# Start addresses of split weights, and a smaller table of cosines and sines, in a hybrid attention layer

## The chip, the cores and the metric

The kernel runs on one core of one Trainium2 chip. The core has TensorE (PE in the profile, with its weight loads shown as PEld), VectorE (DVE), ScalarE (ACT), GpSimd (POOL) and SyncE (SP), which here only issues transfers. The metric is the device time of one execution in microseconds (us). Durations of single instructions are given in ns.

## The reference

One encoder layer on 512 tokens of width 2048, with 16 learned tokens put ahead (528 in all), everything in float32:

```python
hn = rmsnorm(h, pre_norm_g)
proj = hn @ w_in                       # 2048 -> queries, keys, values, gates of A and B
# mixer A: 8 query heads, 2 key/value heads of 128; RMSNorm of q and k, axial rotation, softmax
ya = gqa_axial_mixer(qa, ka, va, ...) * silu(ga)
# mixer B: 8 heads of two 64-wide halves; softmax(s1) - lam * softmax(s2), distance penalty, RMSNorm
yb = diff_attn_mixer(qb, kb, vb, ...) * silu(gb)
y  = concat([ya, yb]) @ w_out
out = (h + rmsnorm(y, post_norm_g))[:, 16:, :]

def rope_half(x, ang):                 # applied to each 64-wide half of a head
    x1, x2 = split(x, 2)               # 32 and 32
    return concat([x1 * cos(ang) - x2 * sin(ang), x2 * cos(ang) + x1 * sin(ang)])
```

## The kernel before

**Products in split form.** Every float32 operand of a large product is held as two rounded parts, high and low: `wh`, `wl` for weights, `xh`, `xl` for the normalised input. A product is three matmuls, high by high, low by high and high by low (`three`). A weight block of 128 x 1024 arrives in `st` by a transfer on SP's queue (`wload`), ACT writes its high part `wh`, and DVE subtracts to get `wl` (`wsplit`). `st`, `wh` and `wl` each have three buffers in pool `wp`. `fetch` keeps two to three blocks ahead of PE, in the order of the list `todo`.

**Projections.** `dense_T` multiplies 128 output columns of the weights (the stationary operand, 128 x 128 a matmul) by all of x (the moving operand), over 16 steps k of the input width. For keys and values the moving operand has all 528 tokens, in two runs of 264 columns (`KEYS`), so one k is six matmuls of 264 columns. For queries of B and gates it has the 512 real tokens in one run (`REAL`), three matmuls of 512 columns a k. The projections of A's queries (`queries_A`) and of the output have the weights as the moving operand. `T_VB`, `T_KB`, `T_KA` and `T_VA` name the blocks of values and keys of B and A in `w_t`; `col` gives the two sources of one block of 128 columns.

**Order.** PE's order is written out by the program: a planner (`Lanes`) counts an estimated time as it emits projections, and lets generators of the attention heads run at set lags in between (scores `sc`, transposes `tr`, products with the values `pv`). The order on ACT and DVE comes from a scheduler that knows priorities: weight splits have `high_priority`. SP's loads stand in program order.

**Places in memory.** Operands lie in SBUF, each partition of which is one row of bytes. In the built program the tiles of x start 192 bytes behind a multiple of 256, so that the keys' two runs start at 192 and 224 and the run of real tokens at 0 (modulo 256); `wh` and `wl` start at 0. The keys of the B heads (`s1`, `s2`, `s` in the profile) have four buffers, at 64, 128, 192 and 0, and their queries (`q`, `l`) start at 64.

**The rotation.** For A, `head_norm` scales each head, and `rope` rotates: x times cosines, plus the exchanged halves of x times sines. The tables `cosT` and `sinT` have 128 columns per token: each value of the 32 cosines of an axis stands twice, and each sine stands once with a minus and once with a plus. `rope` runs twice for the keys of A (`kn`, at 473 and 504 us) and eight times for its queries (`qn`, from 552 to 656 us).

Of the kernel before, what the change touches and what calls it, by code (L numbers as in the profile page):

```python
# [11 lines left out]
F32R = mybir.dt.float32r  # L12
F16 = mybir.dt.float16
AF = mybir.ActivationFunctionType
ALU = mybir.AluOpType
AX = mybir.AxisListType

P = 128
# [5 lines left out]
TT = SEQ // P  # L24
# [16 lines left out]
T_KA, T_VA, T_GA, T_QB, T_KB, T_VB, T_GB = 0, 2, 4, 12, 20, 28, 36  # L41


class Lanes:
# [13 lines left out]
    def mm(self, out, lhsT, rhs, start, stop):  # L58
        n = int(np.prod(rhs.shape[1:]))
        us = max(n, 256) / 2370.0  # L60
        if rhs.dtype == F32:
            us = 4 * max(n, 128) / 2370.0
        self._add(self.nc.tensor.matmul(out, lhsT, rhs, start=start, stop=stop), us)  # L63
# [45 lines left out]
def kernel(ctx: ExitStack, tc: tile.TileContext, xT, xn, xm, w_s, w_t, w_q, w_o,  # L109
                             gpre, gq, gk, lams, gsub, gpost, ident_d, cos_d, sin_d, dist_d, out):  # L110
    nc = tc.nc
# [6 lines left out]
    wp = ctx.enter_context(tc.tile_pool(name="wp", bufs=3))  # L118
# [5 lines left out]
    ap = att.enter_context(tc.tile_pool(name="ap", bufs=2))  # L124
# [6 lines left out]
    def ctile(shape, name, dt=F32, src=None, pool=cst):  # L131
        t = pool.tile(shape, dt, name=name, tag=name, bufs=1)
        if src is not None:
            load(t, src)
        return t
# [5 lines left out]
    def load(out, in_):  # L141

        tc.keep_in_program_order(nc.sync.dma_start(out=out, in_=in_))


    def wload(src, n=1024, dma=nc.sync.dma_start, parts=1):
        st = wp.tile([P, 1024], F32, name="st", tag="st")
        ws = None
        for i in range(parts):
            c = slice(i * n // parts, (i + 1) * n // parts)  # L150
            dma(out=st[:, c], in_=src if parts == 1 else src[:, c])
            ws = wsplit(st, c, ws)
        return ws

    def wsplit(st, c=slice(0, 1024), ws=None):
        wh, wl = ws or [wp.tile([P, 1024], F32R, name=n, tag=n) for n in ("wh", "wl")]
        with tc.high_priority(rank[0]):
            nc.scalar.activation(wh[:, c], st[:, c], AF.Copy)  # L158
            nc.vector.tensor_tensor(out=wl[:, c], in0=st[:, c], in1=wh[:, c].bitcast(F32),  # L159
                                    op=ALU.subtract)  # L160
        return wh, wl
# [35 lines left out]
    todo, chunks = [], []  # L197

    def fetch(ahead=2):
        while todo and len(chunks) <= ahead:  # L200
            src = todo.pop(0)
            chunks.append(src() if callable(src) else wload(src))
        return chunks.pop(0)
# [15 lines left out]
    def col(ct):  # L219
        return [w_t[ct, :, k0:k0 + 8, :] for k0 in (0, 8)]  # L220


    start = [KEYS, REAL, REAL]
    first = [[pd.tile([P, 512], F32, name="pd", tag="pd") for _ in segs] for segs in start]
    for k0 in range(0, KT, 2):
        xload(k0)
        wh, wl = wload(w_s[k0 // 2], 768, load, 2 if k0 == 0 else 1)
        xload(k0 + 1)
        for k in (k0, k0 + 1):
            for i, (segs, pss) in enumerate(zip(start, first)):  # L230
                c = slice((i + 3 * (k - k0)) * P, (i + 3 * (k - k0) + 1) * P)
# [12 lines left out]
                                op0=ALU.mult, op1=ALU.add)  # L244
        nc.gpsimd.tensor_tensor(out=dst, in0=dst, in1=mhalf[:rows, :dst.shape[1]], op=ALU.pow)  # L245

    todo += col(T_VB)
    chunks += [wload(todo.pop(0)) for _ in range(2)]


    ssx = ctile([P, TT, 2], "ssx")
# [3 lines left out]
    for t in range(TT + 1):  # L255
        for j in range(2):
            st = ap.tile([P, 1024], F32, name="xns", tag="ph" if j else "pl")
            rows = P if t < TT else NM
            src = xn[t * P:(t + 1) * P, :] if t < TT else xm
# [12 lines left out]
                            op0=ALU.mult)  # L272
# [3 lines left out]
    def spread():  # L276
# [4 lines left out]
        mm(ps[:, :NM], ones[:NM, :], dg[:NM, :NM], start=True, stop=True)  # L281
        nc.vector.tensor_copy(out=rB[:, :NM], in_=ps[:, :NM])

    cosT = ctile([P, TT, P], "cosT", src=cos_d, pool=ap)
    sinT = ctile([P, TT, P], "sinT", src=sin_d, pool=ap)
    gqB = ctile([P, P], "gqB", src=gq, pool=ap)
    gkB = ctile([P, P], "gkB", src=gk, pool=ap)
    pad(cst, "spad", 160)
# [2 lines left out]
                            op0=ALU.mult)  # L291
# [291 lines left out]
    def head_norm(raw, n, g, rows=P):  # L583

        ss = ap.tile([P, 4], F32, name="ssh", tag="ssh", bufs=4)
        for i in range(n):
            jk = ap.tile([P, P], F32, name="jk", tag="jk", bufs=1)
            nc.scalar.activation(jk[:rows], raw[:, i, :], AF.Square, accum_out=ss[:rows, i:i + 1])  # L588
        rstd(ss[:rows, :n], ss[:rows, :n], P, rows)
        for i in range(n):  # L590
            nc.vector.scalar_tensor_tensor(out=raw[:, i, :], in0=raw[:, i, :],
                                           scalar=ss[:rows, i:i + 1], in1=g[:rows], op0=ALU.mult,
                                           op1=ALU.mult)

    def rope(x, cos, sin):

        t2f = ap.tile([P, NT], F32, name="t2", tag="tT")
        t2 = t2f[:, :4 * P].rearrange("p (n a r) -> p n a r", n=4, a=2)
        xv = x.rearrange("p n (a r) -> p n a r", a=2)
        sv = sin.rearrange("p n (a r) -> p n a r", a=2)  # L600
        nc.vector.tensor_tensor(out=t2[:, :, :, 0:32], in0=xv[:, :, :, 32:64],
                                in1=sv[:, :, :, 0:32], op=ALU.mult)
        nc.vector.tensor_tensor(out=t2[:, :, :, 32:64], in0=xv[:, :, :, 0:32],
                                in1=sv[:, :, :, 32:64], op=ALU.mult)
        nc.vector.tensor_tensor(out=x, in0=x, in1=cos, op=ALU.mult)
        nc.vector.tensor_tensor(out=x, in0=x, in1=t2f[:, :4 * P].rearrange(
            "p (n d) -> p n d", n=4), op=ALU.add)

    def keys_A(pss):
# [8 lines left out]
        def turn():  # L618
            tr = ptr.tile([P, 512], F32, name="tr", tag="tr")
            for c in range(TT):  # L620
                transpose(tr[:, c * P:(c + 1) * P], kf[:, NM + c * P:NM + (c + 1) * P], ident)
            for c in range(TT):
                nc.scalar.activation(kn[:, c, :], tr[:, c * P:(c + 1) * P], AF.Copy,
                                     scale=rt[:, c:c + 1])
            yield LAG["bank"]
            tr = ptr.tile([P, 512], F32, name="tr", tag="tr")
            transpose(tr[:NM, :P], kf[:, 0:NM], ident)
            nc.scalar.activation(km[:, 0, :], tr[:NM, :P], AF.Copy, scale=rm)
            head_norm(kn, TT, gkB)
            head_norm(km, 1, gkB, NM)  # L630
            rope(kn, cosT, sinT)
            yield LAG["rope"]
            tr = ptr.tile([P, 512], F32, name="tr", tag="tr")
            for c in range(TT):
                transpose(tr[:, c * P:(c + 1) * P], kn[:, c, :], ident)
            hi(kh[:, NM:], tr)
            lo(kl[:, NM:], tr, kh[:, NM:])
            yield LAG["bank"]
            tr = ptr.tile([P, 512], F32, name="tr", tag="tr")
            transpose(tr[:, :NM], km[:, 0, :], ident[:NM, :NM])  # L640
            hi(kh[:, :NM], tr[:, :NM])
            lo(kl[:, :NM], tr[:, :NM], kh[:, :NM])
# [3 lines left out]
    def queries_A(g):  # L646

        pss = [pd.tile([P, 512], F32, name="pd", tag="pd") for _ in range(TT)]
        for k0 in range(0, KT, 2):
            wh, wl = fetch()  # L650

            for k, ts in [(k, h) for h in ((0, 1), (2, 3)) for k in (k0, k0 + 1)]:
                c = slice((k - k0) * 512, (k - k0 + 1) * 512)
                for t in ts:
                    ts_ = slice(NM + t * P, NM + (t + 1) * P)
                    mm(pss[t], xh[k][:, ts_], wh[:, c], start=(k == 0), stop=False)
                    mm(pss[t], xl[k][:, ts_], wh[:, c], start=False, stop=False)
                    mm(pss[t], xh[k][:, ts_], wl[:, c], start=False, stop=(k == KT - 1))
                    lanes.poll()
        res = []  # L660
        for t in range(TT):
            tag = "ql" if g == 0 else "fr" if t < 2 else "f"
            qn = ap.tile([P, 4, P], F32, name="qn", tag=tag, bufs=2 if tag == "fr" else 4)
            nc.scalar.activation(qn.rearrange("p n d -> p (n d)"), pss[t], AF.Copy,
                                 scale=rt[:, t:t + 1])
            res.append(qn)

        def turn():
            for t, qn in enumerate(res):
                head_norm(qn, 4, gqB)  # L670
                rope(qn, cosT[:, t:t + 1, :].broadcast_to([P, 4, P]),
                     sinT[:, t:t + 1, :].broadcast_to([P, 4, P]))
                yield LAG["norm"]

        return res, lanes.spawn(turn(), 0.0)


    for h in range(NH):
        if h and h not in LATE:
            todo += col(T_GB + h)  # L680
        if h + 1 < NH:
            todo += col(T_VB + h + 1) + col(T_KB + h + 1) + col(T_QB + h + 1)
    for i in range(2):
        todo += col(T_KA + i) + col(T_VA + i)
    for grp in range(2):
        todo += [w_q[grp, :, k0:k0 + 2, :] for k0 in range(0, KT, 2)]
        for h in GATES[grp]:
# [95 lines left out]
    for grp in range(2):  # L783
        qn, q_task = queries_A(grp)
        for i in range(4):
            h = 4 * grp + i
# [12 lines left out]
    op = ctx.enter_context(tc.tile_pool(name="op", bufs=1, side="right", reuse_waits="tile"))  # L799
# [70 lines left out]
    t1, t2, t3, t4 = [], [], [], []  # L870
# [243 lines left out]
```

## Time and profile before

| What | before |
|---|---|
| median of 3 runs | 928.91 us (928.5 to 929.88) |
| the profiled execution | 928.50 us |
| its span, first to last instruction | 926.7 us |
| mean granted clock of TensorE | 0.998 |
| PE busy, matmuls | 912.6 us, 5498 |
| DVE / ACT / POOL busy | 571.0 / 491.8 / 116.6 us |
| bytes moved by DMA | 128.11 MB |

The profile shows one execution on the chip. The span is 1.8 us shorter than the execution's time. A row of a group gives line, engine, operation, output and inputs by the program's names, partitions x elements, count, then busy us and mean ns, then the idle time of the engine before it and what ended it. A row of the timeline gives start and duration in us; in brackets stands idle time before it. A row of the chain gives start and length of one piece of the work that ended last. `pd`, `po`, `sc`, `tr` and `pv` are sums in PSUM of a projection, of the output projection, of scores, of transposes and of products with values.

### The profile page before, as it was taken

What the parts mean: (1) busy time and instruction counts of PE and PEld (TensorE: products, weight loads), DVE (VectorE), ACT (ScalarE), POOL (GpSimd) and SP (SyncE); (2) the same over time, 40 slices, a digit from 0 to 9 for tenths busy, and PEclk for the clock granted to TensorE, in tenths of its full rate; (3) what the DMA queues carried; (4) which work ended last, traced back from release to release, by engine and by line L of the source; (5) the groups of instructions that cost most, each with busy time, mean ns of one, the idle gap of its engine ahead of it and who ended that gap; (6) DMA issues with size and microseconds to landing.
All of it is one profiled execution on the core that took longest, in us unless ns stands there. A gap on an engine that the chain in (4) does not pass through costs nothing.

```text
span 926.7 us, 14251 instructions
## 1 busy us (share of the span) xinstructions
PE 912.6 (98%) x5498; PEld 807.3 (87%) x5498; DVE 571.0 (62%) x1012; ACT 491.8 (53%) x853; POOL 116.6 (13%) x164
## 2 busy tenths in 40 slices
PE   9999999999999999999999999999999999999996
PEld 7989898998989899898999888887888888888884
DVE  6276675757557486665765236447745574654797
ACT  6765474737456374654754254337555673524661
POOL 0001110110101111010010011114111111200110
PEclk9999999999999999999999999999999999999999
DMA  9755534544636355222223323221222162865884
GB/s 333 261 158 148 137 105 125 156 119 145 160 94 189 94 151 156 69 87 86 80 69 87 106 73 111 69 80 58 76 73 80 57 216 83 274 215 167 299 304 181
DMA packets 43252, 128.11 MB, mean 138 GB/s; under 512 B 5008, under 2 KB 8976, under 8 KB 42928
## 3 DMA queue, kind: packets, MB, share of 16 engines
q1 hardware_dynamic: 39776, 115.66, 37.4%
q0 software_dynamic: 3264, 11.54, 6.7%
q8 instruction: 43, 0.70, 0.3%
q14 instruction: 25, 0.20, 0.1%
q10 hardware_dynamic: 144, 0.01, 0.0%
HBM read 118.80 MB, written 25.17 MB: 155 GB/s over the span
## 4 chain that ended last, share of the span: by engine, by line
PE 90%; DVE 4%; ACT 2%; issue 2%; DMA 1%; POOL 1%; SPq 0%; DVEq 0%; ACTq 0%; POOLq 0%
PE pd L63 58%; PE po L63 16%; PE sc L63 6%; PE tr L66 5%; PE pv L63 5%; DVE y L1003 1%; DVE wl L159 1%; DMA xs<-in_xT_dram 1%; DMA os<-oscr 1%; PE ss L63 0%; DVE l L316 0%; ACT wh L158 0%; POOL ssh L245 0%; ACT jk L588 0%; DVE y L1015 0%
## 5 line engine op out<-in xcount | busy, mean ns | idle before, releaser
L63 PE MATMUL pd<-xh,wh 128*128 128x264 f32 (+1 forms) x992 | 331.9, 335 | 0.6 <-ACT wh L158 0.4
L63 PE MATMUL pd<-xh,wl 128*128 128x264 f32 (+1 forms) x992 | 322.9, 325 | 1.1 <-DVE wl L159 1.0
L63 PE MATMUL pd<-xl,wh 128*128 128x264 f32 (+1 forms) x992 | 322.9, 325 | 0.4 <-DVE xl L185 0.4
L158 ACT ACTIVATE wh<-st 128x1024 fp32r<-128x1024 f32 (+2 forms) x147 | 152.8, 1040 | 206.9 <-issue 89.6
L159 DVE TENSOR_TENSOR wl<-st,wh 128x1024 fp32r<-128x1024 f32 (+2 forms) x147 | 176.5, 1201 | 118.9 <-ACT wh L158 117.8
L63 PEld LDWEIGHTS pd<-xh,wl 128*128 128x128 f32 x992 | 186.4, 188 | 17.5 <-DVE wl L159 1.5
L63 PEld LDWEIGHTS pd<-xh,wh 128*128 128x128 f32 x992 | 186.6, 188 | 12.7 <-ACT wh L158 0.9
L63 PEld LDWEIGHTS pd<-xl,wh 128*128 128x128 f32 x992 | 187.1, 189 | 11.0 <-DVE xl L185 0.8
L476 ACT ACTIVATE p<-p,mx 128x528 f32<-128x528 f32 x64 | 47.0, 734 | 43.9 <-DVE mx L468 43.5
L63 PE MATMUL po<-wh,oh 128*128 128x512 f32 x176 | 69.5, 398 | 0.1
L63 PE MATMUL po<-wh,ol 128*128 128x512 f32 x176 | 68.3, 391 | 0.2 <-DVE ol L316 0.2
L63 PE MATMUL po<-wl,oh 128*128 128x512 f32 x176 | 68.2, 390 | 0.0
L313 ACT ACTIVATE ph<-tr 128x512 fp32r<-128x512 f32 x64 | 37.7, 591 | 37.3 <-PE tr L66 37.1
L468 DVE CUSTOM_DVE_ANT_0 p<-sc,dist 128x528 f32<-128x528 f32 x64 | 44.8, 701 | 14.3 <-PE sc L63 14.1
L316 DVE TENSOR_TENSOR pl<-tr,ph 128x512 fp32r<-128x512 f32 x64 | 43.3, 687 | 15.2 <-ACT ph L313 14.7
L63 PE MATMUL pd<-wh,xh 128*128 128x512 f32 x128 | 51.6, 403 | 0.0
L66 PE MATMUL tr<-ident,p 128*128 128x128 f32 (+1 forms) x320 | 50.6, 272 | 0.1
L63 PE MATMUL pd<-wl,xh 128*128 128x512 f32 x128 | 50.1, 391 | 0.0
L63 PE MATMUL pd<-wh,xl 128*128 128x512 f32 x128 | 50.0, 391 | 0.0
L66 PEld LDWEIGHTS tr<-ident,p 128*128 128x128 f32 (+1 forms) x320 | 37.2, 131 | 11.2 <-DVE pl L316 1.0
L481 POOL TENSOR_SCALAR p<-p,sm 128x528 f32<-128x528 f32 x32 | 23.1, 722 | 170.0 <-DVE sm L478 157.7
L566 POOL TENSOR_SCALAR p<-p,smA 128x528 f32<-128x528 f32 x32 | 23.7, 741 | 145.5 <-DVE smA L565 119.0
(201 smaller groups left out, 1476.9 us busy)
## 6 DMA issues: line engine op xcount, KB each, us to landing
st<-in_w_t_dram SPq DMA_DIRECT2D x82, 512.0 KB, 3.8
st<-in_w_o_dram SPq DMA_DIRECT2D x24, 512.0 KB, 3.8
ws<-in_w_o_dram POOLq DMA_DIRECT2D x16, 512.0 KB, 5.8
st<-in_w_q_dram SPq DMA_DIRECT2D x16, 512.0 KB, 3.6
st<-ws SPq DMA_DIRECT2D x16, 512.0 KB, 4.1
xs<-in_xT_dram SPq DMA_DIRECT2D x16, 264.0 KB, 5.3
xns<-in_xn_dram SPq DMA_DIRECT2D x8, 512.0 KB, 5.3
ws<-in_w_o_dram SPq DMA_DIRECT2D x8, 512.0 KB, 5.1
```

The lines of the kernel that those rows point to most:

```text
L63: self._add(self.nc.tensor.matmul(out, lhsT, rhs, start=start, stop=stop), us)
L66: self._add(self.nc.tensor.transpose(out, in_, ident), 0.109)
L158: nc.scalar.activation(wh[:, c], st[:, c], AF.Copy)
L159: nc.vector.tensor_tensor(out=wl[:, c], in0=st[:, c], in1=wh[:, c].bitcast(F32), op=ALU.subtract)
L313: nc.scalar.activation(dst, src, AF.Copy)
L316: nc.vector.tensor_tensor(out=dst, in0=src, in1=h.bitcast(F32), op=ALU.subtract)
L468: nc.vector.tensor_tensor_reduce(out=two(p), in0=sc[:, :, :HALF], in1=two(dist[:, w0:w0 + NT]), scale=-0.125 / slope(h), scalar=3.0e38, op ...
L476: nc.scalar.activation(p2[m], p2[m], AF.Exp, scale=-1.0, bias=mx[:, m:m + 1], accum_out=sm[:, m:m + 1])
L481: nc.gpsimd.tensor_scalar(out=p2[0], in0=p2[0], scalar1=sm[:, 0:1], scalar2=1.0, op0=ALU.mult, op1=ALU.mult)
L566: nc.gpsimd.tensor_scalar(out=p, in0=p, scalar1=sm, scalar2=1.0, op0=ALU.mult, op1=ALU.mult)
L1003: order(nc.vector.scalar_tensor_tensor(out=v, in0=v, scalar=ry[t], in1=xres[t, g], op0=ALU.mult, op1=ALU.add))
```

## The change

`wh` and `wl` become 1088 columns wide, and of these 1024 are used. For weights of keys and values (`kv`) the used columns start at column 24, that is 96 bytes behind a multiple of 256; for all others at column 0. The first keys of B (`w_s`) stay at 0 too. Three buffers of both tiles take 1536 bytes more in each partition. In exchange `cosT` and `sinT` hold each of the 32 cosines and sines of the two axes once (64 columns per token where there were 128, 2048 bytes less in each partition), loaded in four transfers instead of two. `rope` multiplies by the one table of sines twice, once with a factor of -1, and by the cosines in two instructions.

```diff
-    def wload(src, n=1024, dma=nc.sync.dma_start, parts=1):
+    SHIFT = 24
+
+    def wload(src, n=1024, dma=nc.sync.dma_start, parts=1, shift=0):
...
-            ws = wsplit(st, c, ws)
+            ws = wsplit(st, c, ws, shift)
...
-    def wsplit(st, c=slice(0, 1024), ws=None):
-        wh, wl = ws or [wp.tile([P, 1024], F32R, name=n, tag=n) for n in ("wh", "wl")]
+    def wsplit(st, c=slice(0, 1024), ws=None, shift=0):
+        wh, wl = ws or [wp.tile([P, 1088], F32R, name=n, tag=n)[:, shift:shift + 1024]
+                        for n in ("wh", "wl")]
...
+    def kv(ct):
+        return [lambda src=src: wload(src, shift=SHIFT) for src in col(ct)]
...
-    todo += col(T_VB)
-    chunks += [wload(todo.pop(0)) for _ in range(2)]
+    todo += kv(T_VB)
+    chunks += [todo.pop(0)() for _ in range(2)]
...
-    cosT = ctile([P, TT, P], "cosT", src=cos_d, pool=ap)
-    sinT = ctile([P, TT, P], "sinT", src=sin_d, pool=ap)
+    cosT, sinT = [ctile([P, TT, 2, 32], n, pool=ap) for n in ("cosT", "sinT")]
+    for a in range(2):
+        load(cosT[:, :, a, :], cos_d[:, :, a * 64:a * 64 + 32])
+        load(sinT[:, :, a, :], sin_d[:, :, a * 64 + 32:a * 64 + 64])
...
-        sv = sin.rearrange("p n (a r) -> p n a r", a=2)
-        nc.vector.tensor_tensor(out=t2[:, :, :, 0:32], in0=xv[:, :, :, 32:64],
-                                in1=sv[:, :, :, 0:32], op=ALU.mult)
-        nc.vector.tensor_tensor(out=t2[:, :, :, 32:64], in0=xv[:, :, :, 0:32],
-                                in1=sv[:, :, :, 32:64], op=ALU.mult)
-        nc.vector.tensor_tensor(out=x, in0=x, in1=cos, op=ALU.mult)
+        A, B = slice(0, 32), slice(32, 64)
+        nc.vector.scalar_tensor_tensor(out=t2[:, :, :, A], in0=xv[:, :, :, B], scalar=-1.0,
+                                       in1=sin, op0=ALU.mult, op1=ALU.mult)
+        nc.vector.tensor_tensor(out=t2[:, :, :, B], in0=xv[:, :, :, A], in1=sin, op=ALU.mult)
+        for r in (A, B):
+            nc.vector.tensor_tensor(out=xv[:, :, :, r], in0=xv[:, :, :, r], in1=cos, op=ALU.mult)
...
-            todo += col(T_VB + h + 1) + col(T_KB + h + 1) + col(T_QB + h + 1)
+            todo += kv(T_VB + h + 1) + kv(T_KB + h + 1) + col(T_QB + h + 1)
...
-        todo += col(T_KA + i) + col(T_VA + i)
+        todo += kv(T_KA + i) + kv(T_VA + i)
```

PE's and GpSimd's instructions stand in the same order in both programs. On DVE the order moves at two kinds of places. The first is the start of the attention, about 50 to 60 us in: `kf`, `qf` and `vf` are keys, queries and values of head 0 or 1 taken from PSUM, `s` and `l` their low parts, `gB` the first gate, `lmt`, `lsm`, `nlam` the small work for lambda. DVE before, from the second half of the keys on:

```order
L307 TENSOR_TENSOR kf<-pd,rB 128x264
L302 TENSOR_SCALAR nlam<-nlam 128x1
L341 SCALAR_TENSOR_TENSOR qf<-pd,rB 128x512
L384 TENSOR_TENSOR gB_706<-pd,rB 128x512
L316 TENSOR_TENSOR s_679<-kf,s_679 64x528
L316 TENSOR_TENSOR s_680<-kf,s_680 64x528
L159 TENSOR_TENSOR wl<-st,wh 128x1024
L316 TENSOR_TENSOR l_689<-qf,q_687 64x512
L159 TENSOR_TENSOR wl<-st,wh 128x1024
L316 TENSOR_TENSOR l_690<-qf,q_688 64x512
```

DVE after, the same stretch and what follows it:

```order
L351 SCALAR_TENSOR_TENSOR qf<-pd,rB 128x512
L311 TENSOR_TENSOR nlam<-lsm 128x1
L326 TENSOR_TENSOR s_681<-kf,s_681 64x528
L312 TENSOR_SCALAR nlam<-nlam 128x1
L326 TENSOR_TENSOR s_682<-kf,s_682 64x528
L326 TENSOR_TENSOR l_691<-qf,q_689 64x512 x2
L163 TENSOR_TENSOR wl<-st,wh 128x1024 x2
L326 TENSOR_TENSOR l_692<-qf,q_690 64x512 x2
L317 TENSOR_TENSOR vf<-sc,rB 128x264 x2
L394 TENSOR_TENSOR gB_708<-pd,rB 128x512
```

Two low parts of queries now stand ahead of the first split, and the gate behind the values. ACT at the same place, before:

```order
L299 ACTIVATE lsm<-lsm 128x2
L313 ACTIVATE s_679<-kf 64x528
L313 ACTIVATE s_680<-kf 64x528
L158 ACTIVATE wh<-st 128x1024
L313 ACTIVATE q_687<-qf 64x512
```

ACT after:

```order
L323 ACTIVATE s_681<-kf 64x528
L309 ACTIVATE lsm<-lsm 128x2
L323 ACTIVATE s_682<-kf 64x528
L323 ACTIVATE q_689<-qf 64x512
L162 ACTIVATE wh<-st 128x1024
```

One half of the queries' high part now stands ahead of the first split.

The second kind of place is each rotation. DVE before, in the second group of A's queries near 642 us; `qlA` is the low part of the queries of one head of A, for which PE waits there:

```order
L565 RECIPROCAL smA<-smA 128x1
L601 TENSOR_TENSOR t_6727<-qn,sinT 128x8x32
L316 TENSOR_TENSOR qlA<-tr,qh 128x512
L316 TENSOR_TENSOR pl<-tr,ph 128x512
L603 TENSOR_TENSOR t_6727<-qn,sinT 128x8x32
L591 SCALAR_TENSOR_TENSOR qn<-qn,ssh,gqB 128x128
L605 TENSOR_TENSOR qn<-qn,cosT 128x512
```

DVE after:

```order
L575 RECIPROCAL smA<-smA 128x1
L611 SCALAR_TENSOR_TENSOR t_6736<-qn,sinT 128x8x32
L326 TENSOR_TENSOR qlA<-tr,qh 128x512
L613 TENSOR_TENSOR t_6736<-qn,sinT 128x8x32
L326 TENSOR_TENSOR pl<-tr,ph 128x512
L615 TENSOR_TENSOR qn<-qn,cosT 128x8x32 x2
```

The multiplication by cosines is two instructions, and the rotation's second product stands ahead of `pl`.

More of the change, by code (lines that the diff above doesn't have):

```diff
@@ L670, in turn @@
                 head_norm(qn, 4, gqB)
-                rope(qn, cosT[:, t:t + 1, :].broadcast_to([P, 4, P]),
-                     sinT[:, t:t + 1, :].broadcast_to([P, 4, P]))
+                rope(qn, cosT[:, t:t + 1].broadcast_to([P, 4, 2, 32]),
+                     sinT[:, t:t + 1].broadcast_to([P, 4, 2, 32]))
                 yield LAG["norm"]
```

## The prediction

> **What bounds the kernel now.** I read the page first, then the chain that ended last, then the waits of TensorE (PE), then PE's groups with the shapes kept apart.
>
> ```profile
> span 926.7 us, 14251 instructions
> PE 912.6 (98%) x5498; PEld 807.3 (87%) x5498; DVE 571.0 (62%) x1012; ACT 491.8 (53%) x853; POOL 116.6 (13%) x164
> PE 90%; DVE 4%; ACT 2%; issue 2%; DMA 1%; POOL 1%; SPq 0%; DVEq 0%; ACTq 0%; POOLq 0%
> ...
> PE pd L63 <- DVE wl L159: 1.0, 1, 1.0
> PE tr L66 <- DVE vf L307: 0.6, 1, 0.6
> ...
> PE sc L63 <- DVE qlA L316: 0.4, 1, 0.4
> ```
>
> PE is busy for 98% of the span and has 90% of the chain; the waits shown, 2.0 us together, are those that the change comes near, and no other is over 1.2 us. So time changes here only if PE's matmuls follow each other at another distance, or if one of these few waits grows. How far apart they stand is read from start to start, because a row's duration contains a part that overlaps the next matmul. The rows that carry this come from the groups and from the chain:
>
> ```profile
> L63 PE MATMUL pd<-xh,wh 128*128 128x264 f32 x608 | 177.2, 292 | 0.6 <-ACT wh L158 0.4
> L63 PE MATMUL sc<-xh,wh 128*128 128x264 f32 x32 | 9.2, 289 | 0.0
> ...
> 113.43 2.88 PE pd L63 x24
> 116.81 2.91 PE pd L63 x24
> ...
> 172.33 2.92 PE pd L63 x24
> 175.75 2.92 PE pd L63 x24
> ...
> 790.40 116.31 PE po L63 x513
> ...
> 10.86 0.28 PE L63 MATMUL pd<-xh,wh 128*128 128x264 f32 x1
> ...
> 503.68 0.28 PE L63 MATMUL pd<-xh,wh 128*128 128x264 f32 x1
> ```
>
> The changed weights belong to the projections of 264 columns. Each of x608 stands three times (xh with wh, xl with wh, xh with wl), the x32 of the first values likewise: 3 x 640 = 1920. The start's keys (16 x 2 x 3 = 96) use weights that are not shifted, so 1824 matmuls read shifted weights, 304 groups of six.
>
> The chain shows two speeds for the same six matmuls with the same operands: 2.88 us for 24 (120.0 ns each) and 2.92 us for 24 (121.7 ns). In nanoseconds, the sixes that no other matmul interrupts (226, the first at 10.86 us, the last at 503.68 us) fall on 720 or near 730, mean 727.6, so 121.3 ns per matmul. The output projection, 512 columns and nothing else on PE, takes 116.31 / 513 = 226.7 ns; in proportion to columns 264 would take 116.9 ns. So 4.4 ns of each short matmul is lost to something that the long ones do not show, and the loss depends on a phase.
>
> **Part 1: the shift.** It adds and removes no PE instruction and leaves PE's order as it is. While one matmul streams x, the weights of the next are loaded. I call the start of the moving operand minus that of the next weights, modulo 256 bytes, their distance. In the program before, x starts at 192, the two halves of the keys' columns therefore at 192 and 224, and the weights at 0: distances 192 and 224. With weights at 96 they are 96 and 128. All other tiles keep their place modulo 256.
>
> Before has no projection with weights at 96. The nearest rows are the scores of the B heads, also 264 columns: four matmuls (two halves, two weights), weights at 64, and s in one of four buffers at 64, 128, 192 or 0. A burst is read from its first start to that of the next projection:
>
> ```profile
> 105.95 0.29 PE L63 MATMUL sc<-s,q 128*128 128x264 f32 x1
> ...
> 106.44 0.39 PE L63 MATMUL pd<-xh,wh 128*128 128x512 f32 x1
> ...
> 467.87 0.28 PE L63 MATMUL sc<-s,q 128*128 128x264 f32 x1
> ...
> 468.35 0.29 PE L63 MATMUL pd<-xh,wh 128*128 128x264 f32 x1
> ...
> 64.58 0.28 PE L63 MATMUL sc<-s,q 128*128 128x264 f32 x1
> ...
> 65.06 0.28 PE L63 MATMUL pd<-xh,wh 128*128 128x264 f32 x1
> ...
> 412.29 0.28 PE L63 MATMUL sc<-s,q 128*128 128x264 f32 x1
> ...
> 412.78 0.28 PE L63 MATMUL pd<-xh,wh 128*128 128x264 f32 x1
> ...
> 446.11 0.28 PE L63 MATMUL sc<-s,q 128*128 128x264 f32 x1
> ...
> 446.59 0.39 PE L63 MATMUL pd<-xh,wh 128*128 128x512 f32 x1
> ```
>
> The first pair of bursts are the first and last of 16 with s at 0, so distances 192 and 224, those of the projections now: mean 488.4 ns, 122.1 per matmul. The next pair are the first and last of 16 with s at 192 (distances 128 and 160): mean 485.5, 121.4. The last is the quickest of 12 uninterrupted ones with s at 128 (64 and 96; 476 to 488): mean 481.3, 120.3. The new distances, 96 and 128, lie between the last two classes: (121.4 + 120.3) / 2 = 120.9 against 122.1, a gain of 1.2 ns. Times 1824 that is 2.2 us. It agrees with another way to say it: if the shifted sixes always ran at the quick of the two speeds, they would gain (727.6 - 720) x 304 = 2.3 us. The bursts are short and scatter by 4 ns and more, so this is the weakest term. Its bounds: all sixes at 116.9 ns per matmul, (121.3 - 116.9) x 1824 = 8.0 us gained; all at 123.7, 2.4 x 1824 = 4.4 us lost. The 123.7 is the slowest class of single matmuls in these scores, distance 32, mean of 32; the half of a burst from 61.31 to 61.56 is one of them, 122 and 126 ns:
>
> ```profile
> 61.31 0.28 PE L63 MATMUL sc<-s,q 128*128 128x264 f32 x1
> 61.43 0.29 PE L63 MATMUL sc<-s,l 128*128 128x264 f32 x1
> 61.56 0.28 PE L63 MATMUL pd<-xh,wh 128*128 128x264 f32 x1
> ```
>
> I take -2.2 us, between the ends and by the nearest rows.
>
> The Trainium skill, TensorE: Matmul & The Clock Gate, section Step-by-step: what each phase is for, says PE reads SBUF through two independent ports, one for the moving operand and one for weights. By that rule the start of the weights could not matter, and this term would be zero; the two speeds above are at equal addresses and do not contradict it, the difference of the burst classes does, weakly. The same page, Back-to-back issue gap, gives an isolated matmul N / 2.4 + 2.5 ns; as an estimate 112.5 ns for 264 columns, by which the most to gain would be 16 us; no 264-column stretch of this trace runs that fast.
>
> **Part 2: the rotation.** Ten rotations (2 of keys, 8 of queries) each gain an instruction: one multiplication by cosines over 512 elements becomes two over 256, and one product with sines carries a factor -1.
>
> ```profile
> L601 DVE TENSOR_TENSOR t<-qn,sinT x8: 408/424/427, 552.1 to 652.7; 128x256 f32<-128x256 f32 x8
> ...
> L605 DVE TENSOR_TENSOR qn<-qn,cosT x8: 673/692/994, 552.9 to 655.5; 128x512 f32<-128x512 f32 x8
> ...
> 642.48 0.69 DVE L316 TENSOR_TENSOR qlA<-tr,qh 128x512 fp32r<-128x512 f32 x1
> ```
>
> 2 x 424 - 692 = 156 ns, ten times 1.6 us on DVE. DVE is busy 62% and PE waits for it in this stage once, 0.4 us, for the low part of a head's queries (qlA), with a run of rotations just ahead on DVE. There the extra 156 ns reaches PE: +0.2 us. The product with -1 is put at the price of the plain one (it moves the same elements; if it cost as much as its double, 0.4 us, only the same place would feel it). The other nine are covered by PE's projections, which never wait for DVE there; with that cover gone they would cost 1.4 us.
>
> **Part 3: the loads and the start.** Two loads of 256 KB become four of 64 KB with runs of 128 bytes; behind them in SP's queue stand the small constants and then the second value weights.
>
> ```profile
> 42.50 0.43 SPq L143 DMA_DIRECT2D sinT<-in_sin_dram  x1
> ...
> 45.40 12.29 SPq L151 DMA_DIRECT2D st<-in_w_t_dram  x5
> ...
> L858 SPq DMA_DIRECT2D ts<-oscr x12: 359/360/433, 808.1 to 894.0; - x12
> ...
> st<-in_w_t_dram SPq DMA_DIRECT2D x82, 512.0 KB, 3.8
> ...
> 52.76 1.06 ACT L158 ACTIVATE wh<-st 128x1024 fp32r<-128x1024 f32 x1
> 53.73 1.27 ACT L313 ACTIVATE q<-qf 64x512 fp32r<-64x512 f32 x2
> ...
> 51.96 0.68 DVE L384 TENSOR_TENSOR gB<-pd,rB 128x512 f32<-128x512 f32 x1
> ...
> 54.15 1.23 DVE L159 TENSOR_TENSOR wl<-st,wh 128x1024 fp32r<-128x1024 f32 x1
> ```
>
> Two more issues at 0.43 us put the queue 0.9 us back. The weights issued right behind them, at 45.40 us, land 3.8 us later, at 49.2; ScalarE (ACT) splits them at 52.76. 3.5 us of slack cover the 0.9. If an issue of four times the runs cost four times as much, the delay would be 4 x 1.72 - 2 x 0.43 = 6.0 us and PE would lose up to 2.5 us; but ts, with two runs to a partition where sinT has one, is issued in 0.36 us, so I take no loss.
>
> The order on ACT and DVE moves at this place. On ACT one half of q now stands ahead of the first split (+0.64 us), on DVE two l stand ahead of wl and gB has gone behind vf. PE waits for this wl (the 1.0 us above), so it starts about 0.7 us later. But the wait of 0.6 us for vf, five k further on, goes: vf has one instruction of 0.68 us less ahead of it. Net +0.1 us. What is late next is nothing for PE: gB is needed only by the end of head 0.
>
> **Sum.** The profiled execution took 928.50 us, 0.4 below the median of 928.91. 928.5 - 2.2 + 0.2 + 0.1 = 926.6 us. From no change a measurement of this kernel can tell about 0.2%, 1.9 us; against the median this is a gain of 2.3.
>
> **Rivals.** (a) The address does not choose the speed. For it: both speeds occur at equal distances, and the swap from 192 and 224 to 96 and 128 only exchanges which half is at an odd multiple of 32. Against it: the burst classes. Then 928.5 + 0.3 = 928.8. (b) The distance opens a phase without any loss; every short matmul at 116.9 ns: 928.5 + 0.3 - 8.0 = 920.8. Against it: none of the three classes of bursts comes below 120 ns. (c) Slower: the new distances hold the sixes at a worse stand, the weights' load meeting the stream in each half. For it: the 123.7 above. At 123.7 it is 928.5 + 0.3 + 4.4 = 933.2; from about 122.4 ns per matmul on, 1.1 over now, it decides the sign, past 930.8. The late weights of part 3 at their upper bound would look the same (931.3), but as one wait near 54 us.
>
> **How the numbers follow.** Forecast (modest gain by the quick speed, 925 to 927.0) 0.36, (a) 0.34, (b) or most of it 0.11, (c) 0.19. Faster by over 0.2% is forecast and (b), 0.47; the same is (a), 0.34; slower is (c), 0.19. For 8 in 10 the range leaves out the far half of (b), below 922, and the far half of (c), above 931.5.
>
> **What would show it.** Right: stretches of 24 in the chain at 2.88 us or less throughout instead of up to 2.92, the output's 513 unchanged at 116.31, DVE some 1.6 us busier, the wait for wl near 54 us about 0.7 longer and that for vf gone. Wrong: the same mixture of 2.88 and 2.92 (then a), 2.81 (then b), or over 2.93 (then c).

## The result, and the profile after

The change makes the kernel slower: 933.08 us median of five runs (932.55 to 934.36) against 928.50 of five runs before (928.16 to 929.88), a ratio of 1.0050 with a 95% interval of 1.0038 to 1.0061. That is 4.6 us, outside the predicted range. The profiled execution of the changed kernel took 934.36 us, the longest of the five; 1.35 us of it are explained below by the start of the program and do not belong to the change.

The page of the changed kernel, its engines and its chain:

```profile
span 932.6 us, 14265 instructions
PE 918.9 (99%) x5498; PEld 814.3 (87%) x5498; DVE 571.4 (61%) x1022; ACT 492.1 (53%) x853; POOL 117.3 (13%) x164
PE 94%; DVE 3%; ACT 1%; issue 1%; DMA 0%; DVEq 0%; ACTq 0%
```

The same 5498 matmuls are busy 6.3 us longer, and PE's share of the chain rises from 90% to 94%. DVE, which got ten more instructions, is busy only 0.4 us longer.

The chain of the changed kernel; columns are start, length, engine and number of matmuls. The first four rows are the places that the prediction shows for before:

```profile
116.67 2.93 PE pd L63 x24
120.10 2.95 PE pd L63 x24
...
176.00 2.97 PE pd L63 x24
179.46 2.94 PE pd L63 x24
...
503.03 2.97 PE pd L63 x24
...
796.39 116.31 PE po L63 x513
```

The stretches of 24 matmuls that took 2.88 to 2.92 us take 2.93 to 2.98. The output projection's 513 matmuls of 512 columns take 116.31 us as before: the loss is not spread over all of PE.

PE's groups of the changed kernel, busy us and mean ns of one:

```profile
L63 PE MATMUL pd<-xh,wh 128*128 128x264 f32 x608 | 179.2, 295 | 0.7 <-ACT wh L162 0.7
L63 PE MATMUL pd<-xl,wh 128*128 128x264 f32 x608 | 175.2, 288 | 0.0
L63 PE MATMUL pd<-xh,wl 128*128 128x264 f32 x608 | 174.6, 287 | 1.7 <-DVE wl L163 1.7
L63 PE MATMUL po<-wh,oh 128*128 128x512 f32 x176 | 69.5, 398 | 0.1
```

The first group was at 177.2 us and 292 ns. The last row, output weights that are not shifted, is unchanged from before.

PE's waits in the changed kernel (what was waited for, us in total, times, longest):

```profile
PE pd L63 <- DVE wl L163: 1.7, 1, 1.7
...
PE pd L63 <- ACT wh L162: 0.7, 1, 0.7
PE sc L63 <- DVE qlA L326: 0.4, 1, 0.4
```

The wait for wl went from 1.0 to 1.7 us, the one for vf is gone from the list, the one for qlA stayed at 0.4.

**Where the 4.6 us are.** I compared the start of each matmul with that of the same matmul before; their order is the same, so the drift can be read stage by stage.

```
stage (matmul number)                        drift of the changed kernel, us
start of the program (0 to 300)              +1.35
second value weights (300 to 350, 52-64 us)  +1.55
projections and attention (350 to 3540)      +3.15
end, with the output projection              -0.05
```

The first line is the clock at the program's start. The trace records when TensorE's granted clock goes from half to full: at 10.47 us in this execution, at 4.48 us in that of before. Until then matmuls of 512 columns stand 427 ns apart, behind it 227:

```profile
6.97 0.63 PE L63 MATMUL pd<-xh,wh 128*128 128x512 f32 x1
7.39 0.63 PE L63 MATMUL pd<-xl,wh 128*128 128x512 f32 x1
```

Over the experiments below, this line lies between -0.8 and +1.32 us against the same execution of before, with no relation to the shift or the loads, so it differs from execution to execution. The two lines behind it add to 4.70 us, against 4.58 between the medians. Of the third line, 3.42 us lie in the 1569 steps from one 264-column projection matmul to the next; all other steps of this stage together are 0.27 us shorter than before.

### The profile page after: what moved, and what is told of

It reads as the page before. It is cut to its first block, busy times and chain, and to the rows that moved or that the text cites. A ratio compares the mean times of both kernels' runs of the same rounds, so it can differ in the third digit from the quotient of the medians.

```text
span 932.6 us, 14265 instructions
## 1 busy us (share of the span) xinstructions
PE 918.9 (99%) x5498; PEld 814.3 (87%) x5498; DVE 571.4 (61%) x1022; ACT 492.1 (53%) x853; POOL 117.3 (13%) x164
## 4 chain that ended last, share of the span: by engine, by line
PE 94%; DVE 3%; ACT 1%; issue 1%; DMA 0%; DVEq 0%; ACTq 0%
PE pd L63 61%; PE po L63 16%; PE sc L63 7%; PE pv L63 5%; PE tr L66 5%; DVE y L1013 1%; DVE wl L163 0%; PE ss L63 0%; ACT jk L598 0%; DMA gcol<-in_gpre_dram 0%; DVE l L326 0%; DVE y L1025 0%; ACT wh L162 0%; ACT qn L674 0%; DVE y L1019 0%
## 5 line engine op out<-in xcount | busy, mean ns | idle before, releaser
L63 PEld LDWEIGHTS pd<-xh,wh 128*128 128x128 f32 x992 | 188.3, 190 | 12.7 <-ACT wh L162 1.2
L576 POOL TENSOR_SCALAR p<-p,smA 128x528 f32<-128x528 f32 x32 | 26.5, 827 | 142.6 <-DVE smA L575 114.5
```

The source lines that it names most:

```text
L576: nc.gpsimd.tensor_scalar(out=p, in0=p, scalar1=sm, scalar2=1.0, op0=ALU.mult, op1=ALU.mult)
```

## The experiments

Two things could hold the loss: the distance between moving operand and weights in the 264-column matmuls (theory D in the expectations), and what happens at the start, 52 to 64 us, where the four smaller loads changed the order on ACT and DVE. The first four kernels take shift and loads apart and then ask whether it is the distance or the place that counts.

**e1: the shift undone, all else as changed.**

```diff
-    SHIFT = 24
+    SHIFT = 0
```

> The changed kernel with all weights at distance offset 0 again (tiles still 1088 wide, small tables, four loads kept). Theory D (the distance of x from the next weights sets the loss): interrupted-free sixes of 264 columns go from 740 back to about 728 ns, the stretch at half clock near 58 us stays, so about 933.1 - 3.0 = 930.1 us. Theory S (the start alone, with its half clock, makes the loss, and the speed of the sixes is chance): sixes stay mixed near 740, about 933 us.

Measured: 929.65 us, ratio to before 1.0017 (1.0007 to 1.0026). The chain of e1 has the old lengths again:

```profile
114.48 2.88 PE pd L63 x24
117.85 2.91 PE pd L63 x24
...
173.38 2.92 PE pd L63 x24
```

The uninterrupted sixes (the six matmuls of one step k, with no other between them) are at 727.7 ns (222 of them; 727.6 before, 740.3 in the changed kernel), and matmuls 350 to 3540 drift by 0.01 us. So the shift alone holds that part. But matmuls 300 to 350 are still 1.55 us late. What is there shows in the timeline of PE in the changed kernel (start, duration; in brackets idle time before it and what ended it):

```profile
55.48 0.39 PE L63 MATMUL pd<-xh,wh 128*128 128x264 f32 x1 [0.66 <-ACT wh L162]
55.71 0.28 PE L63 MATMUL pd<-xl,wh 128*128 128x264 f32 x1
57.73 0.39 PE L63 MATMUL pd<-xh,wl 128*128 128x264 f32 x1 [1.74 <-DVE wl L163]
...
58.59 0.42 PE L63 MATMUL pd<-xl,wh 128*128 128x264 f32 x1
58.81 0.42 PE L63 MATMUL pd<-xh,wl 128*128 128x264 f32 x1
59.03 0.42 PE L63 MATMUL pd<-xh,wh 128*128 128x264 f32 x1
...
61.23 0.42 PE L63 MATMUL pd<-xl,wh 128*128 128x264 f32 x1
61.45 0.38 PE L63 MATMUL pd<-xh,wl 128*128 128x264 f32 x1
61.67 0.29 PE L63 MATMUL pd<-xh,wh 128*128 128x264 f32 x1
```

Behind the two waits, the matmuls stand 220 ns apart instead of 120, from 58.25 to 61.67 us. The windows of the three kernels give the granted clock of such a stretch (PE, PEld, DVE, ACT and POOL busy with their counts, then the clock as a share of full speed, DMA share and GB/s); first the changed kernel:

```profile
57.00:61.50 4.50, 3.77 (x19) 3.77 (x20) 4.42 (x7) 3.78 (x5) 0.00 (x0) 0.64 0.56 173
```

The same window of before:

```profile
57.00:61.50 4.50, 3.93 (x32) 3.53 (x31) 4.36 (x7) 3.84 (x5) 0.00 (x0) 1.00 0.70 218
```

And of e1, one microsecond earlier, where its late weights stand:

```profile
56.00:60.50 4.50, 4.50 (x25) 4.50 (x26) 4.42 (x7) 3.58 (x4) 0.00 (x0) 0.62 0.66 214
```

19 matmuls are recorded where before had 32, with a clock of 0.64 in the mean instead of 1.00. By the trace's clock records the half clock lasted 3.413 us in the changed kernel and 3.41 us in e1 (56.62 to 60.03). The Trainium skill, TensorE: Matmul & The Clock Gate, What's actually happening, states a window of 4096 cycles at 1.2 GHz, 3413 ns, that runs freely; the measured length agrees. The Trainium skill, TensorE: Matmul & The Clock Gate, Why this matters for your kernels, asks for no idle gap over about 3 us; here gaps of 0.66 and 1.74 us within 3 us were enough, while the 0.4 and 1.05 us of before were not.

The traces show more of the rule. In all fourteen, each stretch of full clock in the records is a whole number of 3.413 us (14 of them from 10.47 to 58.25 us in the changed kernel, 269 in before). Counted on that grid, TensorE's rows leave it idle for 2.38 us of the stretch from 54.84 to 58.25 us, just ahead of the half clock, and for 2.15 us of that ahead of it in e1. In the twelve other traces no such stretch up to 900 us has more than 1.46 us of idle time, and none is followed by the half clock. So the idle time seems to be summed over a fixed stretch, and it matters whether a boundary falls between two gaps; that was not tried apart. The twelve times of e1 lie between 927.65 and 931.27 us, five of them above 930.7; it may be that not every execution has the half clock, as would follow if a boundary can fall between the gaps, but only one of them has a profile.

**e2: one transfer a table, the shift kept.** The tables are still held once; only the loading is undone, and with it the scheduler's order on ACT and DVE at the start, which becomes that of before: in the traces ACT's order is the same throughout, and DVE's up to the first rotation.

```diff
-    for a in range(2):
-        load(cosT[:, :, a, :], cos_d[:, :, a * 64:a * 64 + 32])
-        load(sinT[:, :, a, :], sin_d[:, :, a * 64 + 32:a * 64 + 64])
+    load(cosT.rearrange("p t a r -> p (t a) r"),
+         cos_d.rearrange("p t (a r) -> p (t a) r", a=2)[:, :, 0:32])
+    load(sinT.rearrange("p t a r -> p (t a) r"),
+         sin_d.rearrange("p t (a r) -> p (t a) r", a=2)[:, :, 32:64])
```

> The changed kernel with the shift of 96 bytes kept, but each small table fetched by one transfer of 3 dimensions instead of two; the built order of ACT and DVE at the start is then that of before. Theory D: the sixes stay near 740 ns, the wait for the first wl falls from 1.7 to about 1.0 us, the half clock near 58 us is gone, so 933.1 - 1.6 = 931.5 us. Theory S: about 928.7 us.

Measured: 931.27 us, 1.0033 (1.0021 to 1.0045). Matmuls 300 to 350 drift by -0.02 us, and PE's waits are those of before:

```profile
PE pd L63 <- DVE wl L163: 1.0, 1, 1.0
PE tr L66 <- DVE vf L316: 0.5, 1, 0.5
```

The slow sixes stay, 740.3 ns (225 of them), and the projections drift by 3.10 us. The chain of e2:

```profile
113.47 2.93 PE pd L63 x24
116.90 2.95 PE pd L63 x24
...
172.80 2.97 PE pd L63 x24
```

**e3: both undone; the rotation and the small tables alone.** The edits of e1 and e2 together.

> Shift 0 and one transfer for each small table: of the change only the rotation's extra instruction and the small tables are left. Theory D: sixes at 728 ns, no half clock, 928.5 + 0.2 = 928.7 us. Theory S: 928.7 us as well; if the rotation's 1.6 us of DVE reach PE, up to 930.

Measured: 928.22 us, 1.0003 (0.9994 to 1.0011). The rotation with its ten more instructions, the smaller tables and the wider weight tiles cost nothing that can be measured. Sixes 727.6 ns (227), projections +0.05 us. The chain of e3:

```profile
112.67 2.88 PE pd L63 x24
116.04 2.91 PE pd L63 x24
...
171.56 2.92 PE pd L63 x24
```

With e3 as the base, the shift costs 931.27 - 928.22 = 3.05 us and the four loads 929.65 - 928.22 = 1.43 us. 928.50 + 3.05 + 1.43 = 932.98; measured is 933.08. The two parts add: about two thirds of the loss are the shift's, a third the start's. That they add to within 0.1 us is partly luck, since e1's interval alone (1.0007 to 1.0026) is 1.8 us wide.

**e4: distances as before, every place moved.** In e2, `x` moves by 96 bytes modulo 256 too, and all weights that meet it are shifted; the output weights are not. (The larger pad moves `x` down by 160 bytes, from 192 to 32 modulo 256, so with weights at 96 the distances are 192 and 224 again. In plain bytes they are 256 less than in e3.)

```diff
-    def wload(src, n=1024, dma=nc.sync.dma_start, parts=1, shift=0):
+    def wload(src, n=1024, dma=nc.sync.dma_start, parts=1, shift=SHIFT):
...
-    pad(xp, "xpad", 32)
+    pad(xp, "xpad", 192)
...
+    todo += [lambda src=src: wload(src, shift=0) for src in out_w]
```

> Two loads of the tables as in e2, and now x and all weights that meet x are moved by 96 bytes, so every distance of a projection is that of before (192 and 224 for keys and values, 0 for the rest), while the split still writes its results at 96. Theory D: sixes at 728 ns, 928.7 us as e3. Rival theory W (it is the place of the weights, or the writes of ACT and DVE to it, not the distance): sixes at 740 or more, 931.5 us or more.

Measured: 929.29 us, 1.0014 (1.0006 to 1.0023). The shifted weights are back at the old speed, 728.4 ns for six (226). The chain of e4:

```profile
113.51 2.88 PE pd L63 x24
116.87 2.92 PE pd L63 x24
...
172.62 2.92 PE pd L63 x24
```

Theory W needed 740 or more. So it is not the weights' place modulo 256, nor writing them there, that costs the 12.7 ns a six; the distance to x does. The projections still drift by 0.94 us. By the trace 0.35 us of it lie in the steps between 264-column projection matmuls (3.42 in e2) and 0.43 us in those between 512-column ones, though their distances are those of before; scores, transposes and the changes between kinds add only 0.17. So a small price of the place itself is not ruled out, and what makes the 0.94 us stays open.

**e5 to e12: the other distances.** All have e2's loads, and another shift. Two theories stood against each other first: the loss repeats every 64 bytes (P64), or every 256, with a price for each single distance (P256). After e5 to e8, a third: the price belongs to the pair of distances that alternate (Q).

```diff
-    SHIFT = 24
+    SHIFT = 16      # e5; 32 in e6, 48 in e7, 56 in e8, 8 in e9, 40 in e10, 4 in e11, 60 in e12
```

> As e2 and e3 (one transfer a table), shift 64 bytes: distances 128 and 160. Theory P64 (the loss repeats every 64 bytes): a shift of 64 is no shift, sixes at 728 ns, 928.2 us. Theory P256 (each distance modulo 256 has its own price, as single matmuls show it: 128 at 121.5 to 122.8 ns, 160 at 120.3 to 120.8): sixes at 726 to 730 ns, 928 to 928.5 us.

> Shift 128 bytes: distances 64 and 96. P64: sixes at 728 ns, 928.2 us. P256 (64 at 120.2 ns, 96 at 121.8 to 123.8): sixes at 726 to 732 ns, 928 to 929.5 us.

> Shift 192 bytes: distances 0 and 32. P64: sixes at 728 ns, 928.2 us. P256 (0 at 120.1 to 120.6 ns, 32 at 123.7 to 124.6): sixes near 733 ns, 929.8 us.

> Shift 224 bytes: distances 224 and 0. P64: this is a shift of 32 modulo 64 as 96 is, so sixes at 740 ns and 931.3 us. P256 (224 at 120.5 to 121.6 ns, 0 at 120.1 to 120.6): the cheapest pair, sixes near 724 ns, 927.1 us.

> Shift 32 bytes, one transfer a table: distances 160 and 192. If each distance had its own price (theory P256), 160 at 120.3 to 122.4 and 192 at 120.9 ns: sixes 724 to 730 ns. Theory Q (the price belongs to the pair and its order in time, and can't be put together from single distances): any value between 720 and 745 ns.

> Shift 160 bytes: distances 32 and 64. P256 (32 at 121.0 to 124.5, 64 at 121.7 ns as e6 shows it): sixes 728 to 738 ns. Q: any value between 720 and 745 ns.

> Shift 16 bytes, half of the step used so far: distances 176 and 208. If the loss changes smoothly with the distance, sixes lie between those of shift 0 (727.6) and of shift 32 bytes; if it goes by lines of 32 bytes or more, they are those of shift 0.

> Shift 240 bytes, that is 16 bytes less than none: distances 208 and 240. Smooth: between 727.2 (shift 224) and 727.6 (shift 0), so 727 ns and 928.2 us; if steps of 16 bytes matter by themselves, another value, and under 722 ns this would be the fastest version, 927 us or less.

Measured. The pair are the distances of the two halves of the keys' columns; a six is the mean of six uninterrupted matmuls; the single prices are means over all such matmuls in the stream, so they do not add to the six exactly; the drift is that of matmuls 350 to 3540. e9 to e12 have one run each, beside one of before at 927.65 us.

```
shift B  pair      six ns  single ns       drift us  time us (ratio to before)
0   e3   192/224   727.6   120.9 / 121.7    0.05     928.22  1.0003 (0.9994-1.0011)
16  e11  176/208   729.5   122.0 / 121.1    0.88     929.39
32  e9   160/192   729.1   121.7 / 121.3    0.38     928.71
64  e5   128/160   732.1   121.3 / 122.4    1.33     929.67  1.0008 (0.9998-1.0017)
96  e2    96/128   740.3   123.9 / 122.95   3.10     931.27  1.0033 (1.0021-1.0045)
128 e6    64/96    730.2   121.7 / 122.2    0.76     928.99  1.0003 (0.9994-1.0013)
160 e10   32/64    729.3   122.0 / 120.7    0.43     928.49
192 e7     0/32    729.7   122.0 / 121.0    0.78     929.19  1.0005 (0.9995-1.0014)
224 e8   224/0     727.2   121.65 / 120.7   0.28     928.50  0.9996 (0.9986-1.0005)
240 e12  208/240   731.1   122.2 / 121.2    0.85     929.19
```

(The single prices of shift 0 are from before, those of shift 96 from the changed kernel.) The chain of e8, by the six the best of the nine shifts that are not 0:

```profile
113.25 2.91 PE pd L63 x24
116.65 2.90 PE pd L63 x24
...
172.20 2.91 PE pd L63 x24
```

P64 falls: 96 is 32 modulo 64, but so are 32, 160 and 224, and these are at 727 to 729 ns where it needed 740. The ranges expected of P256 were missed at 64, 192 and 224 bytes (e5, e7, e8) and met at 32, 128 and 160. As a price for each single distance it falls too: the distance 96 costs 123.9 ns beside 128 and 122.2 beside 64; 128 costs 122.95 beside 96 and 121.3 beside 160. So the price depends on the pair, as Q has it; Q allowed any value between 720 and 745 ns, so it is what is left over and not a theory that passed a test. Nor is the course smooth: at 240 bytes a six takes 731.1 ns where its neighbours at 224 and 0 have 727.2 and 727.6, and at 16 bytes 729.5 where 0 and 32 have 727.6 and 729.1. Of ten shifts, 96 bytes is the worst by 8 ns a six, and none is measurably faster than before: the best, 224 bytes, has an interval of 0.9986 to 1.0005. The two speeds of before are seen in its 2.88 and 2.92; e8 runs between them.

Open remains why the pair 96 and 128 is bad: none of these runs shows what goes on in the memory. Open is also what keeps the 264-column matmuls at 119 ns or more in the mean of a six (the quickest uninterrupted one of all traces took 714 ns), when the 226.7 ns of 512 columns would make 116.9.

## Why the prediction was wrong, point by point

- **What bounds the kernel:** right. The time moved only through the distance between short matmuls and through waits between 52 and 64 us. The output's 513 stayed at 116.31 us.
- **Part 1, the shift: -2.2 us forecast, +3.05 measured (e2 against e3). This is the step that failed.** It priced the new distances by the bursts of four scores: 121.4 ns for 128 and 160, 120.3 for 64 and 96, and 120.9 for what lies between, 1.2 less than the 122.1 of 192 and 224. In the long stream the dearest of the three is the cheapest: 121.3 ns per matmul at 192 and 224 (727.6 / 6), 121.7 at 64 and 96 (e6), 122.0 at 128 and 160 (e5); only the order of the last two is that of the bursts. And the middle was not between its neighbours: 96 and 128 is at 123.4 (740.3 / 6). Two assumptions were made without a row for either: that a burst prices the stream, and that the price runs smoothly from one pair to the next. (740.3 - 727.6) x 304 = 3.9 us is an upper end, since many sixes are interrupted; 3.42 us came out between neighbouring matmuls, 3.15 for the stage. With 3.05 in this place and the other terms as forecast the sum is 931.85 us; the 1.2 us that are still missing belong to part 3. What the prediction said about this term being the weakest was right, and its upper bound of +4.4 us held.
- **The Trainium skill's two ports:** by the rule that moving operand and weights are read independently (TensorE: Matmul & The Clock Gate, Step-by-step: what each phase is for), the start of the weights would not matter. e2 and e3 differ in that start alone and are 12.7 ns a six apart. The measurement decides: start addresses matter here, whatever the ports do.
- **Part 2, the rotation: +0.2 us forecast, nothing measured (e3, 1.0003).** The wait for qlA stayed at 0.4 us. DVE's busy time grew by 0.4 us and not 1.6, at least in part since durations of successive instructions overlap. In the timeline of DVE in the changed kernel, the instruction of 0.42 us is followed 0.33 us later by the next, and two multiplications by cosines together take 0.76 us where one of double size took 0.69 (the median before):

```profile
649.23 0.42 DVE L613 TENSOR_TENSOR t<-qn,sinT 128x256 f32<-128x256 f32 x1
649.56 0.69 DVE L326 TENSOR_TENSOR pl<-tr,ph 128x512 fp32r<-128x512 f32 x1
650.16 0.76 DVE L615 TENSOR_TENSOR qn<-qn,cosT 128x256 f32<-128x256 f32 x2
```

- **Part 3, loads and start: +0.1 us forecast, +1.43 measured (e1 against e3).** The order on ACT and DVE did what was read from it: matmul by matmul, the wait for wl adds 0.70 us (0.7 forecast) and that for wh 0.25, and what hung on vf is gone (-0.72 at the wait, -0.28 in the three transposes behind it). Here are the instructions ahead of both, from the timelines of ACT and DVE in the changed kernel:

```profile
53.85 0.64 ACT L323 ACTIVATE q<-qf 64x512 fp32r<-64x512 f32 x1
54.39 1.04 ACT L162 ACTIVATE wh<-st 128x1024 fp32r<-128x1024 f32 x1
...
55.03 1.38 DVE L326 TENSOR_TENSOR l<-qf,q 64x512 fp32r<-64x512 f32 x2
56.45 2.36 DVE L163 TENSOR_TENSOR wl<-st,wh 128x1024 fp32r<-128x1024 f32 x2
```

  The three changes sum to -0.05 us, so the sum of waits was nearly right. What it lacked is what two longer gaps close together do to the clock: one stretch of 3.413 us at half speed, about 16 matmuls at 220 ns instead of 120, 1.6 us; with it the stage comes to the 1.55 of the drift. The queue itself was mis-sized as well, with no consequence. The small tables' first issue takes 1.50 us and the others 0.62 to 0.64 (1.27 and 0.43 for the two large ones before), and gqB behind them 0.62 where it took 0.43. The second weights are issued 3.1 us later than before (45.40 us); 1.1 us of that was there ahead of the tables, so the loads make 2.0, where 0.9 was forecast. The 3.5 us of slack still covered it. From the timeline of SP's queue in the changed kernel:

```profile
43.82 0.62 SPq L143 DMA_DIRECT2D sinT<-in_sin_dram  x1
...
45.16 0.64 SPq L143 DMA_DIRECT2D sinT<-in_sin_dram  x1
...
48.46 10.70 SPq L154 DMA_DIRECT2D st<-in_w_t_dram  x5
```

- **The rivals:** (c), given 0.19, is what happened to the shift, with 123.4 ns instead of its 123.7, and its 933.2 us lies 0.1 from the measured median. That is partly chance: it priced the shift at +4.4 us, which is 3.05, and all else at +0.3, of which the start alone is 1.43. Its sign of recognition, stretches of 24 over 2.93 us, is what the chain shows (2.93 to 2.98). Its reason, that the weights' load meets the stream, no run shows. (a) and (b) are ruled out by e2 against e3.

## What to carry to other kernels

Where one engine is busy 98% and its instructions stand at a pace that the shape does not explain, the pace is worth measuring in the stream itself, from start to start over groups with the same operands; here short bursts put the cheapest of three address pairs last. An address shift is one constant: try several, with the rest of the change held fixed, before building a layout on one value. And a load that is split for the sake of a table can move a scheduler's order elsewhere, so a wait that grows by 0.7 us should be asked for what it does to the clock, not only for its length.

## What the runs showed of the hardware that was not expected

- The pace of back-to-back fp32r matmuls of 264 columns depends on the start of the moving operand against that of the next weights, modulo 256: 121.2 to 123.4 ns over ten shifts, and a distance costs differently beside another one (96 bytes: 123.9 ns beside 128, 122.2 beside 64).
- Two gaps of 0.66 and 1.74 us within 3 us halved TensorE's clock for 3.413 us in the middle of a program in which TensorE is busy 99%; gaps of 0.4 and 1.05 us at the same place did not. Full clock lasts a whole number of 3.413 us, and the half clock followed only where such a stretch held 2.15 us of idle time or more (1.46 at most elsewhere).
- A small load was not issued faster than a large one: 64 KB with runs of 128 bytes took 1.50 us for the first and 0.62 to 0.64 for the three behind it, 256 KB before 1.27 and 0.43. The unchanged load of gqB behind them took 0.62 instead of 0.43, so the price is not of a load's own runs alone.
